# A two-layer encoder trunk with expert retrieval on one core: second-half activations stored in three parts, 20 dense up blocks in place of 26, first splits and gates moved, copies spread

## The chip, the cores and the metric

One core of a Trainium2 chip runs the whole trunk. The metric is the device time of one execution in microseconds; three executions give a median. Its engines work beside each other, each in the order of its own instructions: TensorE (PE in the profile, PEld for its weight loads), VectorE (DVE), ScalarE (ACT), GpSimd (POOL) and SyncE (SP), which here only issues transfers. Sixteen DMA engines carry the transfers.

## The reference, cut to what matters

```python
for i in range(2):                                 # x: 256 tokens x 1024
    m = mla_mixer(x) if i == 0 else dsa_mixer(x)
    x = layernorm(ALPHA * x + m)
    f = peer(x, w_q[i], sub_keys[i], w_down[i], w_up[i])
    x = layernorm(ALPHA * x + f)

def peer(x, w_q, sub_keys, w_down, w_up):          # 16384 experts, 8 heads x 16 picked per token
    s1, s2 = scores of the two halves of x @ w_q against 128 sub-keys each
    expert, gate = top 16 of the 16 x 16 sums of the best 16 of s1 and of s2, softmax
    a = x . w_down[expert]                         # one dot product per token and picked expert
    return sum over picked of gelu(a) * gate * w_up[expert]
```

The 16384 experts are 128 blocks of 128. A token picks at most 128 of 16384.

## The kernel before, in words

**Number format.** Every float32 operand is split in two float16 parts, a high one and the rest (`hi`, `lo` for weights, `xh`, `xl` for activations, made by `Split.high` on ScalarE, L151, and `Split.low` on VectorE, L160). A product is three matmuls, hi·hi, hi·lo and lo·hi. All 128x1024 weight blocks come through one `Stream` in the order of use: `_load` (L199) issues the transfer (a "raw" buffer of a ring of six, on SyncE), then high, then low, some blocks ahead of TensorE.

**Stages of one PEER layer.** The queries (`pq`) and scores (`ps`); the choice of experts on VectorE (`choose`, in pieces between other work); the *down* stage, in which all 128 blocks of `w_down` are multiplied with all 256 tokens (tile `d`, two blocks per step, 24 matmuls of 256 columns each per block) and gelu is put into `A`, a tile [128, 128 blocks, 256 tokens]; and the *up* stage (tile `y`, matmuls of 512 columns).

**Gates.** In the down stage, once the choice is known, `gates` (L1313) turns it, and then 64 groups of four tokens are worked off while the blocks go on: `prepare` (L1380) makes one-hot tiles `hot` on VectorE and `gate` (VectorE or GpSimd and ScalarE), `place` (L1393) multiplies them on TensorE (tile `G`) and multiplies the result into `A` for the four tokens. The same loop counts in `seen` which of the rare blocks are used by which tokens.

**The up stage is not dense.** The first `DENSE` = 26 blocks of `w_up` are multiplied with all tokens. The other 102 (`RARE`) are not: for each of the 128 expert places of a block, the rows of `w_up` that any token of this place uses are listed (`lists`), and 128 rows, one per place, are gathered by an indirect transfer from a DRAM table that holds the row of `w_up` and the 256 activations beside it. 44 such listed items serve both halves of the tokens (12 matmuls of 512 columns each, `JB` + `TB` = 32 + 12), 48 one half (6 matmuls each, `JO` = 24 for each half). `_up_order` sets the order: 20 dense blocks (`HEAD`), then the listed items, with the other 6 dense blocks between them.

**How the table is filled.** The rows of `w_up` are copied from input to table (DRAM to DRAM, 512 KB each, `copies` at L409) behind other loads on SyncE. The activations of the rare blocks are stored by `store` (L1527), four blocks a transfer, in two halves: tokens 0 to 127 from the 32nd group on, tokens 128 to 255 from the 64th group on, which is the end of the down stage. A gather needs the lists, all copies and all stores; its nine buffers also lie on part of `A`, which must have been stored.

**Order.** A scheduler orders the instructions of each engine by its own estimate of times; `tc.issue_after` and the chains of `link` (L455) pin some of it. Transfers issued on SyncE go in order, and each waits until the eighth one before it has landed. `middle_loads` (L1625) fetches the operands of the layer norm (x, gain and bias) half-way through the up items.

Of the kernel before, what the change touches and what calls it, by code (L numbers as in the profile page):

```python
# [16 lines left out]
ALU = mybir.AluOpType  # L17
AX = mybir.AxisListType

P = 128  # L20
T = 256
D = 1024
# [4 lines left out]
NKEYS = 128  # L27
# [38 lines left out]
LEAST, MOST, ROW, SMALL = 64.0, 2.0 ** 40, 4.0, 2.0 ** -24  # L66
BOTH, MOSTLY = 128, 1120
CHECKS = 7 * P
DENSE, HEAD = 26, 20
RARE = P - DENSE  # L70
JB, JO, TB, ROWTAIL = 32, 24, 12, 32
BOTHS = JB + TB
WIDE = D + T
FETCHED, DEEP = 9, 8
LISTED = BOTHS + 2 * JO
END = 6
# [86 lines left out]
class Stream:  # L163
# [35 lines left out]
    def _load(self, upto):  # L199
        while self.n_loaded <= min(upto, len(self.blocks) - 1):  # L200
            src, w, _ = self.blocks[self.n_loaded]
            if self.n_loaded in self.early:
                t = self.early[self.n_loaded]
            elif self.n_loaded in self.rows:
                table, at = self.rows[self.n_loaded]
                t = self.place()
                self.nc.gpsimd.indirect_dma_start(t, None, table, bass.IndirectOffsetOnAxis(ap=at, axis=0))  # L207
# [125 lines left out]
def tile_trunk(ctx: ExitStack, tc: tile.TileContext, ins, out: bass.AP, short, shared):  # L333
    nc = tc.nc
    half = F16 if short else F32R
# [54 lines left out]
    if short:  # L390
        table = [dram.tile([(RARE + 1) * P, WIDE], F32, tag=f"table{i}", name=f"table{i}") for i in range(DEPTH)]
# [17 lines left out]
    def copies(li):  # L409

        down = len(ws.blocks) - NKEYS
        first, few = ((8, 42), (down - 44, 54))[li]
        for n in range(RARE + 1):
            i = first + (down - first) * n // few if n < few else down + 92 * (n - few) // (RARE + 1 - few)
            ws.copied.setdefault(i, []).append((table[li][n * P : (n + 1) * P, :D], ins["up"][li][(DENSE + n) % NKEYS]))

    def add_up(li):
# [91 lines left out]
    def load_x(ar, src):  # L509
        xs = [ar.take(D), ar.take(D)]  # L510
        for t in range(2):
            nc.sync.dma_start(xs[t], src[t])
        return xs

    def rows(o4, lhs, blk, start, stop, tiles=(0, 1)):
# [237 lines left out]

    begun = {}

    def load_affine(ar, li, which):
        g, b = ar.take(D), ar.take(D)
        nc.sync.dma_start(g, ins["ln_gain"][li, which].partition_broadcast(P))
        nc.sync.dma_start(b, ins["ln_bias"][li, which].partition_broadcast(P))
        return g, b  # L760

    def rope(o, p, cos, sin, half, tmp):
# [427 lines left out]
    def peer(li):  # L1190
# [189 lines left out]
        def prepare(g4, engine):  # L1380
            hot = ohp.tile([P, 2, P, 4], F16, tag="V", name="hot")
            gate = ohp.tile([P, 2, 4, P], F16, tag="U", name="gate")
            four = slice(4 * g4, 4 * g4 + 4)
            nc.vector.tensor_tensor(hot, iota4[:, None].to_broadcast([P, 2, P, 4]),  # L1384
                                    place16[:, :, None, four].to_broadcast([P, 2, P, 4]), op=ALU.is_equal)
            engine.tensor_tensor(gate[:, 0], hot[:, 1].rearrange("p c j -> p j c"),  # L1386
                                 gate16[:, four, None].to_broadcast([P, 4, P]), op=ALU.mult)
            for j in range(4):
                t = 4 * g4 + j
                nc.scalar.mul(gate[:, 1, j, :], hot[:, 1, :, j], rest[:, t : t + 1])  # L1390
            onehot[g4] = hot, gate
# [130 lines left out]
                            op0=ALU.mult, op1=ALU.add))  # L1522
            rows_of(up_tail, tail)

        stored = [DENSE, DENSE]

        def store(half, upto):  # L1527

            b0 = stored[half]
            b1 = min(b0 + CHUNKED, NKEYS)  # L1530
            if b0 < b1 <= upto:
                ts = slice(half * P, (half + 1) * P)
                cols = slice(D + half * P, D + (half + 1) * P)
                rows_of = table[li][(b0 - DENSE) * P : (b1 - DENSE) * P, cols].rearrange("(b a) t -> a b t", a=P)
                nc.sync.dma_start(rows_of, A[:, b0:b1, ts])  # L1535
                stored[half] = b1
# [9 lines left out]
        def cut(n):  # L1546
            if n >= len(PAIRED):
                return
            i = PAIRED[n]
            k, slot = ITEMS[i][1], slice(SLOTS[i], SLOTS[i] + 2)  # L1550
            hh, al = xh[:, slot, :], xl[:, slot, :]
            total = split.total("most")
            act(lambda: split.high(hh, A[:, k : k + 2, :], A_UNIT))
            dve(lambda: split.low(al, A[:, k : k + 2, :], A_UNIT, hh, total))
            for j in range(2):
                made[i + j] = hh[:, j, :], al[:, j, :]
# [6 lines left out]
        for b0 in range(0, NKEYS, 2):  # L1563
# [5 lines left out]
                ready = ready or spend(PACE)  # L1569
            if b0 == 0:  # L1570
                chains["pe"] = None
            if short and b0 == NKEYS - 2:
                cut(0)
            t0 = 4 * groups
            if t0 < T:
                nc.scalar.activation(A[:, b0 : b0 + 2, t0:], pv[:, :, t0:], AF.Gelu, scale=1.0 / unit)
# [12 lines left out]
                    prepare(prepared, nc.gpsimd if want == 1 else nc.vector)  # L1589
                    prepared += 1  # L1590
            if short:
                if groups >= 32:
                    store(0, b0)
                    store(0, b0)
                if groups == 64:
                    if listing[0] is None:
                        chains["dve"] = None
                        listing[0] = lists()
                    if b0 < NKEYS - 2:
                        list_on(5)  # L1600
                    for _ in range(3):
                        store(1, b0)
        assert groups == 64, groups
        if not short:
            chains.pop("pe")
# [17 lines left out]
        held = []  # L1623

        def middle_loads():  # L1625
            held.append(load_x(lnar, keep))
            held.append(load_affine(lnar, li, 1))
            if last and short:
                least()
                split.seen = BOTH + split.n["most"]  # L1630
                weigh_up(0, 0, split.seen)

        if short:
            for i, (_, _, tiles) in enumerate(ITEMS):
# [8 lines left out]
                    chains.pop("dve")  # L1643
                    chains.pop("pe")
                if i < HEAD - 8:
                    store(0, NKEYS)
                    store(1, NKEYS)
                    store(1, NKEYS)
                if i == HEAD - 8:
                    assert stored == [NKEYS, NKEYS] and not ws.due, stored  # L1650
                    ws.pieces = 2
                    ws.DMA_AHEAD = DEEP
                if i == len(ITEMS) - 9:
# [176 lines left out]
```

## Time and profile before

| | |
|---|---|
| three runs | 1602.08, 1604.54 (median), 1605.96 us |
| profiled execution | 1601.35 us, of which the program's span is 1599.5 us |
| granted TensorE clock, mean | 0.994 |
| TensorE busy | 1557.4 us (97%) |
| VectorE, ScalarE, GpSimd busy | 1369.6, 1089.2, 379.6 us |
| DMA | 484.28 MB, 303 GB/s on average |
| layer 0: down stage begins, ends | 146 us, 523 us |
| layer 1: down stage ends, last up matmul begins | 1332 us, 1587 us |

Busy time counts a matmul from its start to its modelled end, and neighbours overlap; so the pace of TensorE is read from the number of matmuls in a stretch, and its stalls from stretches in which busy time is short of the stretch.

### The profile page before, as it was taken

To read this page: it belongs to the slowest core of one execution; us is meant where nothing else is said; L and a number is where in the kernel's file an instruction comes from. 1 tells how busy PE (TensorE), PEld (TensorE's weight loads), DVE (VectorE), ACT (ScalarE), POOL (GpSimd) and SP (SyncE) were. 2 spreads that over 40 slices of the span, in tenths; PEclk is the share of its full clock that TensorE was granted. 3 is DMA by queue.
4 is the path that set the end of the run, shared out by engine and by line. 5 is a ranking of instruction groups with operands and counts; after the bars stand their busy time and mean duration, and the time that the engine had idled before them with its cause. 6 is when DMAs were issued, how large, how long until landed. Compare 5 with 4: busy or idle time off the path is not lost.

```text
span 1599.5 us, 33693 instructions
## 1 busy us (share of the span) xinstructions
PE 1557.4 (97%) x12323; PEld 1141.5 (71%) x12323; DVE 1369.6 (86%) x3833; ACT 1089.2 (68%) x1973; POOL 379.6 (24%) x315
## 2 busy tenths in 40 slices
PE   9899999999999999999999999999999999999997
PEld 7669888899999444444578598888999995344443
DVE  7669999999998779878788789989999997698785
ACT  7666666698886457666587667646988873476663
POOL 2001244300000136554032012434000000364440
PEclk9999999999999999999999999999999999999998
DMA  9999889986864999998499998879867659998891
GB/s 378 409 358 361 298 320 331 354 307 209 257 209 155 343 384 374 332 327 326 150 415 408 398 325 291 304 274 323 288 221 229 231 178 277 407 360 311 305 337 51
DMA packets 174447, 484.28 MB, mean 303 GB/s; under 512 B 15040, under 2 KB 68544, under 8 KB 174272
## 3 DMA queue, kind: packets, MB, share of 16 engines
q1 hardware_dynamic: 147488, 360.92, 63.0%
q0 software_dynamic: 26496, 120.60, 20.6%
q8 instruction: 98, 1.61, 0.4%
q14 instruction: 77, 0.63, 0.1%
q10 hardware_dynamic: 288, 0.52, 0.1%
HBM read 450.79 MB, written 139.20 MB: 369 GB/s over the span
## 4 chain that ended last, share of the span: by engine, by line
PE 76%; DVE 11%; DMA 6%; issue 2%; SPq 2%; ACT 2%; DVEq 0%; POOL 0%; POOLq 0%; ACTq 0%
PE d L475 30%; PE y L475 26%; DVE lo L160 6%; PE pq L475 4%; DMA raw<-in_up 4%; PE G L475 4%; PE q L475 3%; PE v L475 2%; PE seen L475 1%; SPq L1535 1%; PE s L475 1%; PE qw L475 1%; ACT hi L151 1%; PE ps L475 1%; DVE arena L1309 1%
## 5 line engine op out<-in xcount | busy, mean ns | idle before, releaser
L475 PE MATMUL d<-xh,lo 128*128 128x256 f16 x2048 | 558.3, 273 | 3.0 <-DVE lo L160 3.0
L475 PE MATMUL d<-xl,hi 128*128 128x256 f16 x2048 | 558.2, 273 | 0.0
L475 PE MATMUL d<-xh,hi 128*128 128x256 f16 x2048 | 558.2, 273 | 0.0
L160 DVE SCALAR_TENSOR_TENSOR lo<-raw,hi 128x1024 f16<-128x1024 f32 (+1 forms) x386 | 473.2, 1235 | 78.9 <-ACT hi L151 73.5
L475 PEld LDWEIGHTS <-hi 128*128 128x128 f16 x5016 | 488.3, 98 | 57.7 <-issue 1.2
L151 ACT ACTIVATE hi<-raw 128x1024 f16<-128x1024 f32 (+1 forms) x366 | 380.7, 1049 | 215.2 <-PE d L475 83.5
L207 POOL DMA_INDIRECT arena<-table,up_at x160 | 179.8, 1124 | 678.7 <-DMA arena<-x 507.4
L475 PEld LDWEIGHTS <-xh 128*128 128x128 f16 x1776 | 172.8, 98 | 211.0 <-issue 8.2
L160 DVE SCALAR_TENSOR_TENSOR lo<-arena,hi 128x512 f16<-128x512 f32 (+1 forms) x366 | 248.4, 716 | 48.2 <-ACT hi L151 47.0
L475 PEld LDWEIGHTS <-lo 128*128 128x128 f16 x2508 | 245.5, 98 | 33.8 <-DVE lo L160 4.9
L475 PE MATMUL y<-hi,xl 128*128 128x512 f16 x816 | 245.5, 380 | 9.2 <-DVE xl L160 9.2
L475 PE MATMUL y<-lo,xh 128*128 128x512 f16 x816 | 246.7, 380 | 2.0 <-DVE lo L160 0.8
L475 PE MATMUL y<-hi,xh 128*128 128x512 f16 x816 | 245.9, 380 | 2.6 <-ACT hi L151 2.6
L151 ACT ACTIVATE hi<-arena 128x1024 f16<-128x1024 f32 x192 | 201.0, 1053 | 39.1 <-issue 21.2
L1390 ACT ACTIVATE gate<-hot,rest 128x128 f16<-128x128 f16 x512 | 167.8, 405 | 13.0 <-DVE hot L1384 10.9
L475 PEld LDWEIGHTS <-xl 128*128 128x128 f16 x888 | 86.2, 98 | 117.8 <-DVE xl L160 14.6
L151 ACT ACTIVATE xh<-arena 128x256 f16<-128x256 f32 (+2 forms) x214 | 87.5, 414 | 86.8 <-PE y L475 61.7
L260 POOL TENSOR_TENSOR lo<-raw,hi 128x1024 f16<-128x1024 f32 x27 | 61.6, 2283 | 192.8 <-ACT hi L258 147.5
L1384 DVE TENSOR_TENSOR hot<-iota,place 128x1024 f16<-128x1024 f16 x128 | 87.6, 689 | 17.1 <-PE G L475 17.0
L160 DVE SCALAR_TENSOR_TENSOR xl<-arena,xh 128x256 f16<-128x256 f32 (+2 forms) x216 | 91.9, 428 | 7.3 <-ACT xh L151 6.9
L475 PE MATMUL G<-gate,hot 128*128 128x128 f16 x1024 | 90.7, 219 | 3.8 <-DVE gate L1386 3.8
L475 PEld LDWEIGHTS <-hot 128*128 128x128 f16 x1536 | 87.8, 113 | 5.0 <-DVE gate L1386 4.3
(261 smaller groups left out, 1811.6 us busy)
## 6 DMA issues: line engine op xcount, KB each, us to landing
raw<-in_down SPq DMA_DIRECT2D x256, 512.0 KB
table<-in_up SPq DMA_DIRECT2D x206, 512.0 KB
raw<-in_up SPq DMA_DIRECT2D x52, 512.0 KB
table<-arena SPq DMA_DIRECT2D x100, 256.0 KB
raw<-in_peer_q SPq DMA_DIRECT2D x24, 512.0 KB
raw<-in_dsa_qk SPq DMA_DIRECT2D x16, 512.0 KB
raw<-in_mla_w_o SPq DMA_DIRECT2D x8, 512.0 KB
arena<-in_peer_q SPq DMA_DIRECT2D x8, 512.0 KB
```

The lines of the kernel that those rows point to most:

```text
L151: return nc.scalar.copy(o, src) if unit == 1.0 else nc.scalar.mul(o, src, unit)
L160: return nc.vector.scalar_tensor_tensor(o, src, unit, hi, op0=ALU.mult, op1=ALU.subtract, accum_out=total)
L207: self.nc.gpsimd.indirect_dma_start(t, None, table, bass.IndirectOffsetOnAxis(ap=at, axis=0))
L260: nc.gpsimd.tensor_tensor(lo, raw, hi if short else hi.bitcast(F32), op=ALU.subtract)
L475: return pe(lambda: nc.tensor.matmul(o, l, r, start=start, stop=stop, skip_group_check=True))
L1309: dve(lambda: nc.vector.tensor_reduce(exp_[t][:, h - 1, :], held, axis=AX.X, op=ALU.add))
L1384: nc.vector.tensor_tensor(hot, iota4[:, None].to_broadcast([P, 2, P, 4]), place16[:, :, None, four].to_broadcast([P, 2, P, 4]), op=ALU.is_ ...
L1390: nc.scalar.mul(gate[:, 1, j, :], hot[:, 1, :, j], rest[:, t : t + 1])
L1535: nc.sync.dma_start(rows_of, A[:, b0:b1, ts])
```

## The change

Seven edits.

1. `DENSE` 26 to 20, `TB` 12 to 16: 20 dense blocks, all ahead of the listed items; 48 items for both halves, 48 for one; 108 rare blocks with a copy and a store each. The up stage has 116 items in place of 118.
2. The activations are stored in four parts (`PARTS`): tokens 0 to 127, 128 to 191, 192 to 223 and 224 to 255, each as soon as its tokens are placed. A stored row is 512, 256, 128 and 128 bytes long.
3. `middle_loads` issues its four transfers on GpSimd's queue, behind the gather that was issued last.
4. The split of the first two dense blocks' activations (`cut(0)`) is issued when the 64th group is placed, and into a spare tile in place of a slot of `xh` and `xl`, which the down stage still reads.
5. The one-hot tiles of groups 1 to 3 wait until the first `gate` has been issued.
6. Copies: fewer ahead of the down stage (24 in place of 42 in layer 0, 46 in place of 54 in layer 1), the others over 108 blocks of the down stage in place of 92.
7. At the end of the down stage three steps of `lists` go with each step in place of five.

```diff
-DENSE, HEAD = 26, 20
+DENSE, HEAD = 20, 20
-JB, JO, TB, ROWTAIL = 32, 24, 12, 32
+JB, JO, TB, ROWTAIL = 32, 24, 16, 32
+PARTS = (0, 128), (128, 192), (192, 224), (224, 256)
...
-        first, few = ((8, 42), (down - 44, 54))[li]
+        first, few = ((12, 24), (down - 44, 46))[li]
...
-            i = first + (down - first) * n // few if n < few else down + 92 * (n - few) // (RARE + 1 - few)
+            i = first + (down - first) * n // few if n < few else down + 108 * (n - few) // (RARE + 1 - few)
...
+            with ExitStack() as order:
+                if short and 0 < g4 < 4:
+                    order.enter_context(tc.issue_after(begun["gate"]))
+                nc.vector.tensor_tensor(hot, iota4[:, None].to_broadcast([P, 2, P, 4]),
+                                        place16[:, :, None, four].to_broadcast([P, 2, P, 4]), op=ALU.is_equal)
...
+            if g4 == 0:
+                begun["gate"] = ins.ins
...
-        def store(half, upto):
+        def store(part, upto):
...
-                ts = slice(half * P, (half + 1) * P)
-                cols = slice(D + half * P, D + (half + 1) * P)
+                ts = slice(*PARTS[part])
+                cols = slice(D + ts.start, D + ts.stop)
...
+            if n == 0:
+                four = spare16.rearrange("p (a b) -> p a b", b=T)
+                hh, al = four[:, 0:2, :], four[:, 2:4, :]
...
-            if short and b0 == NKEYS - 2:
-                cut(0)
...
-                if groups >= 32:
-                    store(0, b0)
-                    store(0, b0)
+                for part, (_, upto) in enumerate(PARTS):
+                    if 4 * groups >= upto:
+                        for _ in range(2 if part == 0 else 3):
+                            store(part, b0)
                 if groups == 64:
                     if listing[0] is None:
                         chains["dve"] = None
+                        cut(0)
                         listing[0] = lists()
                     if b0 < NKEYS - 2:
-                        list_on(5)
-                    for _ in range(3):
-                        store(1, b0)
+                        list_on(3)
...
         def middle_loads():
-            held.append(load_x(lnar, keep))
-            held.append(load_affine(lnar, li, 1))
+            with ExitStack() as order:
+                if short:
+                    order.enter_context(tc.issue_after(ws.fetched))
+                engine = nc.gpsimd if short else nc.sync
+                held.append(load_x(lnar, keep, engine))
+                held.append(load_affine(lnar, li, 1, engine))
```

**The end of layer 0's down stage on SyncE.** In the order before, `128x4x128` is a store of four blocks for 128 tokens. The ten stores in the third row are one of the first half and nine of the second:

```order
L210 DMA raw_7441<-in_up 128x1024
L210 DMA raw_7526<-in_up 128x1024
L1535 DMA table_119<-arena 128x4x128 x10
L210 DMA raw_7556<-in_up 128x1024
L1535 DMA table_119<-arena 128x4x128 x2
L210 DMA raw_7602<-in_up 128x1024
L1535 DMA table_119<-arena 128x4x128 x9
L210 DMA raw_7632<-in_up 128x1024
L1535 DMA table_119<-arena 128x4x128
L210 DMA raw_7676<-in_up 128x1024
L1535 DMA table_119<-arena 128x4x128
L1535 DMA table_119<-arena 128x2x128
```

Now, around the second part, of which the burst begins behind the 48th group (`128x4x64` is a store for 64 tokens):

```order
L1542 DMA table_119<-arena 128x4x128
L1542 DMA table_119<-arena 128x4x64 x9
L212 DMA raw_6875<-in_down 128x1024
L212 DMA raw_6905<-in_down 128x1024
L1542 DMA table_119<-arena 128x4x64 x7
L212 DMA raw_6989<-in_down 128x1024
L1542 DMA table_119<-arena 128x4x64 x3
```

And now behind the 64th group (`128x4x32` is a store for 32 tokens; a like burst of the third part stands between these two pieces, behind the 56th group):

```order
L1542 DMA table_119<-arena 128x4x128
L1542 DMA table_119<-arena 128x4x64
L1542 DMA table_119<-arena 128x4x32 x10
L212 DMA raw_7601<-in_up 128x1024
L1542 DMA table_119<-arena 128x4x32
L212 DMA raw_7648<-in_up 128x1024
L1542 DMA table_119<-arena 128x4x32 x7
L212 DMA raw_7678<-in_up 128x1024
L1542 DMA table_119<-arena 128x4x32
L212 DMA raw_7722<-in_up 128x1024
L1542 DMA table_119<-arena 128x4x32
L1542 DMA table_119<-arena 128x4x128
```

What was one burst of full-width stores behind the 64th group is three bursts, the first two of them among the last loads of the down stage; the last has rows a quarter as long, and x, gain and bias are gone from this queue.

**The first gates on VectorE.** Before, in layer 0:

```order
L1331 TENSOR_TENSOR place_102<-arena 128x256
L1384 TENSOR_TENSOR hot<-iota_106,place_102 128x1024 x4
L1386 TENSOR_TENSOR gate<-hot,gate_103 128x512
L160 SCALAR_TENSOR_TENSOR lo_4048,sums<-raw_3837,hi_4047 128x1024
L1386 TENSOR_TENSOR gate<-hot,gate_103 128x512 x3
```

And now:

```order
L1333 TENSOR_TENSOR place_102<-arena 128x256
L1389 TENSOR_TENSOR hot<-iota_106,place_102 128x1024
L1391 TENSOR_TENSOR gate<-hot,gate_103 128x512
L1389 TENSOR_TENSOR hot<-iota_106,place_102 128x1024 x2
L161 SCALAR_TENSOR_TENSOR lo_4039,sums<-raw_3827,hi_4038 128x1024
```

The first `gate`, which TensorE's first `G` needs, stands behind one `hot` in place of four.

**The first mixer's attention on VectorE.** L812 is the mask and row maximum of the scores `s`; the rows with `lo` split weight blocks (raw_377 and raw_417 those of the values, raw_450 and later ones the mixer's output weights). Before:

```order
L160 SCALAR_TENSOR_TENSOR lo_571,sums<-raw_377,hi_570 128x1024
L781 TENSOR_TENSOR arena<-arena 64x2x256 x2
L160 SCALAR_TENSOR_TENSOR lo_620,sums<-raw_417,hi_619 128x1024
L160 SCALAR_TENSOR_TENSOR lo_656,sums<-raw_450,hi_655 128x1024
L160 SCALAR_TENSOR_TENSOR lo_716,sums<-raw_488,hi_715 128x1024
L160 SCALAR_TENSOR_TENSOR lo_735,sums<-raw_534,hi_734 128x1024
L160 SCALAR_TENSOR_TENSOR lo_955,sums<-raw_574,hi_954 128x1024
L812 ISA arena,m<-s_679,arena 128x128
L812 ISA m 128x1
L812 ISA arena,m<-s_682,arena 128x256
```

And now:

```order
L783 TENSOR_TENSOR arena<-arena 64x2x256 x2
L161 SCALAR_TENSOR_TENSOR lo_725,sums<-raw_526,hi_724 128x1024
L161 SCALAR_TENSOR_TENSOR lo_944,sums<-raw_566,hi_943 128x1024
L814 ISA arena,m<-s_669,arena 128x128
L814 ISA m 128x1
L814 ISA arena,m<-s_672,arena 128x256
L814 ISA m 128x1
L161 SCALAR_TENSOR_TENSOR lo_948,sums<-raw_615,hi_947 128x1024
```

No line of this stage was edited: the scheduler moved the splits, since fewer copies stand ahead of the weights' loads. Before, ScalarE made `hi_734` and `hi_954`, which the last two splits ahead of L812 need, behind its four copies of the values `v`; now the `hi` of every split that stands ahead of the first L812 (L814 in the changed file) comes ahead of these copies.

More of the change, by code (lines that the diff above doesn't have):

```diff
@@ L206, in _load @@
                 t = self.place()
-                self.nc.gpsimd.indirect_dma_start(t, None, table, bass.IndirectOffsetOnAxis(ap=at, axis=0))
+                self.fetched = self.nc.gpsimd.indirect_dma_start(t, None, table,
+                                                                 bass.IndirectOffsetOnAxis(ap=at, axis=0)).ins
             else:
@@ L507, in unscale, with load_x @@
         return nc.scalar.mul(o, p, 1.0 / unit) if short else nc.scalar.copy(o, p)
-    def load_x(ar, src):
+    def load_x(ar, src, engine=nc.sync):
         xs = [ar.take(D), ar.take(D)]
         for t in range(2):
-            nc.sync.dma_start(xs[t], src[t])
+            engine.dma_start(xs[t], src[t])
         return xs
@@ L754, in tile_trunk, with load_affine @@
     begun = {}
-    def load_affine(ar, li, which):
+    def load_affine(ar, li, which, engine=nc.sync):
         g, b = ar.take(D), ar.take(D)
-        nc.sync.dma_start(g, ins["ln_gain"][li, which].partition_broadcast(P))
-        nc.sync.dma_start(b, ins["ln_bias"][li, which].partition_broadcast(P))
+        engine.dma_start(g, ins["ln_gain"][li, which].partition_broadcast(P))
+        engine.dma_start(b, ins["ln_bias"][li, which].partition_broadcast(P))
         return g, b
@@ L1383, in prepare @@
             four = slice(4 * g4, 4 * g4 + 4)
[L1384 to L1387, printed above, removed]
+            with ExitStack() as order:
[3 more added lines that the diff above has]
+                                        place16[:, :, None, four].to_broadcast([P, 2, P, 4]), op=ALU.is_equal)
+            ins = engine.tensor_tensor(gate[:, 0], hot[:, 1].rearrange("p c j -> p j c"),
+                                       gate16[:, four, None].to_broadcast([P, 4, P]), op=ALU.mult)
+            if g4 == 0:
+                begun["gate"] = ins.ins
             for j in range(4):
@@ L1523, in lists @@
             rows_of(up_tail, tail)
-        stored = [DENSE, DENSE]
-        def store(half, upto):
-            b0 = stored[half]
+        stored = [DENSE] * len(PARTS)
+        def store(part, upto):
+            b0 = stored[part]
             b1 = min(b0 + CHUNKED, NKEYS)
             if b0 < b1 <= upto:
-                ts = slice(half * P, (half + 1) * P)
-                cols = slice(D + half * P, D + (half + 1) * P)
+                ts = slice(*PARTS[part])
+                cols = slice(D + ts.start, D + ts.stop)
                 rows_of = table[li][(b0 - DENSE) * P : (b1 - DENSE) * P, cols].rearrange("(b a) t -> a b t", a=P)
                 nc.sync.dma_start(rows_of, A[:, b0:b1, ts])
-                stored[half] = b1
+                stored[part] = b1
         listing = [None]
@@ L1645, in peer @@
                 if i < HEAD - 8:
-                    store(0, NKEYS)
-                    store(1, NKEYS)
-                    store(1, NKEYS)
+                    for part in range(len(PARTS)):
+                        store(part, NKEYS)
+                    store(part, NKEYS)
                 if i == HEAD - 8:
-                    assert stored == [NKEYS, NKEYS] and not ws.due, stored
+                    assert stored == [NKEYS] * len(PARTS) and not ws.due, stored
                     ws.pieces = 2
```

## The prediction

> **What bounds the kernel.** I read the page's busy shares and slices first, then a table of stretches, then who waits for whom where TensorE is short.
>
> ```profile
> PE 1557.4 (97%) x12323; PEld 1141.5 (71%) x12323; DVE 1369.6 (86%) x3833; ACT 1089.2 (68%) x1973; POOL 379.6 (24%) x315
> PE   9899999999999999999999999999999999999997
> DMA  9999889986864999998499998879867659998891
> PE 76%; DVE 11%; DMA 6%; issue 2%; SPq 2%; ACT 2%; DVEq 0%; POOL 0%; POOLq 0%; ACTq 0%
> ```
>
> TensorE is busy nearly everywhere and carries 76% of the chain that ended last. So a matmul less is time less, wherever TensorE does not wait. The table of stretches says where it waits (us of the stretch, then busy us of PE, PEld, DVE, ACT, POOL, then clock, DMA share, GB/s):
>
> ```profile
> 36.00:62.00 26.00, 20.37 (x118) 15.40 (x118) 19.90 (x57) 20.07 (x40) 3.32 (x3) 0.87 1.03 411
> 140.00:300.00 160.00, 159.55 (x1460) 142.75 (x1459) 155.06 (x465) 102.61 (x127) 61.48 (x39) 1.00 0.90 316
> 300.00:320.00 20.00, 18.34 (x187) 16.44 (x186) 19.27 (x40) 14.67 (x32) 0.00 (x0) 1.00 1.00 392
> 412.00:517.00 105.00, 105.00 (x1165) 96.37 (x1163) 96.07 (x171) 83.17 (x217) 0.00 (x0) 1.00 0.67 215
> 517.00:582.00 65.00, 57.63 (x303) 28.96 (x301) 43.96 (x137) 26.80 (x36) 11.71 (x9) 1.00 1.01 358
> 600.00:760.00 160.00, 160.00 (x748) 72.57 (x746) 134.92 (x508) 111.19 (x162) 83.65 (x76) 1.00 0.92 339
> 1040.00:1100.00 60.00, 57.41 (x521) 50.30 (x519) 54.97 (x136) 33.40 (x42) 27.13 (x19) 1.00 0.82 283
> 1100.00:1120.00 20.00, 17.88 (x170) 15.84 (x169) 19.90 (x38) 10.69 (x21) 3.67 (x2) 1.00 0.98 349
> 1320.00:1400.00 80.00, 73.57 (x411) 37.86 (x408) 56.59 (x176) 35.19 (x51) 14.86 (x13) 0.98 0.97 343
> ```
>
> TensorE is short by 5.6 us in the first mixer's attention (36 to 62), 1.7 and 2.1 us where the gates begin (300 to 320, 1100 to 1120), 2.6 us in layer 1's down stage, and 7.4 and 6.4 us where the down stage gives way to the up stage (517 to 582, 1320 to 1400). In the listed part of the up stage (600 to 760) it never waits, with the DMA engines at 0.92. The releasers, from the waits of 240 to 320, 36 to 62, 515 to 600 and 1318 to 1400 in this order (engine and line, what it waited for: us, times, longest):
>
> ```profile
> PE G L475 <- DVE gate L1386: 1.7, 1, 1.7
> ...
> PE s L475 <- DVE m L812: 4.5, 1, 4.5
> ...
> ACT hi L151 <- DMA raw<-in_up: 31.2, 12, 7.5
> PE y L475 <- DVE xl L160: 4.7, 4, 2.5
> ...
> ACT hi L151 <- DMA raw<-in_up: 31.7, 12, 7.3
> PE y L475 <- DVE xl L160: 4.5, 3, 2.5
> ```
>
> **Fewer dense blocks.** Per layer 6 dense items of 12 matmuls go and 4 listed items of 12 come: 24 matmuls of 512 columns less, 48 in both layers. Their pace is in the stretch of tile y alone, and the two rows behind it price 6 more columns of `seen`:
>
> ```profile
> 600.00:760.00 160.00, 159.96 (x742) 0.00 (x0) 1.00 0.92 339
> ...
> L475 PE MATMUL G<-gate,hot x1024: 219/219/247, 312.5 to 1321.5; 128*128 128x128 f16 x171
> ...
> L475 PE MATMUL seen<-gate,hot x512: 208/208/208, 312.6 to 1321.4; 128*128 128x102 f16 x171
> ```
>
> 159.96 / 742 = 0.2156 us each: -10.35 us. 26 columns are 11 ns, 6 are 2.5 ns, times 512: +1.3 us. That holds if gathers keep up. Before, 184 gathers and 12 interleaved dense loads feed the listed parts; now 192 gathers of 640 KB in a stretch that is 3% shorter, so some 345 GB/s for 339, where 411 GB/s stands in the first row of the table. I cost it at nothing. Splits are cover here too: VectorE has 134.92 of 160 us, and per item nothing changes.
>
> **First gates.** VectorE's timeline at 309 us:
>
> ```profile
> 309.38 2.50 DVE L1384 TENSOR_TENSOR hot<-iota,place 128x1024 f16<-128x1024 f16 x4
> 311.79 0.68 DVE L1386 TENSOR_TENSOR gate<-hot,gate 128x512 f16<-128x512 f16 x1
> ```
>
> Three of four `hot` move behind the gate: 3 x 0.6 = 1.8 us, against idles of 1.7 and 2.1 us. Taken: -1.7 and -1.8, -3.5 us.
>
> **Early first split.** The longest wait of `y` for `xl` is 2.5 us in each layer: the first `xh` can be written only when the last `d` has read its slot. With the spare tile it is made some blocks sooner: -5.0 us, hidden in VectorE's time before the stage's end (96.07 of 105 us). The fewer list steps there make room.
>
> **Stores in parts.** Behind the wait for `xl`, the rest of the shortfall, 4.9 + 3.9 = 8.8 us, is loads of dense up blocks that come late (31 us of ScalarE's waits in each layer). Their cause is the burst of stores:
>
> ```profile
> DMA packets 13733, 8.67 MB, mean 299 GB/s; under 512 B 463, under 2 KB 13216, under 8 KB 13731
> ...
> table<-arena SPq DMA_DIRECT2D x26, 256.0 KB
> raw<-in_up SPq DMA_DIRECT2D x5, 512.0 KB
> ```
>
> This is 517 to 546 us: 29 x 16 = 464 engine-us. 515 packets of 4 KB at 411 GB/s over 16 engines are 159 ns each, 82 us; the rest, over 13216 rows of 512 bytes, is 28.5 ns a row: 0.91 us per store, 23.7 us for 26. 512 bytes at that rate are 20 ns, so a straight line says 8.6 ns plus bytes: 18.6 ns for 256, 13.6 ns for 128 bytes, 0.60 and 0.44 us per store. No row shows a short row written to DRAM; the ends are by bytes alone (10 and 5 ns) and as dear as 512 bytes (28.5). I take the line, as two sizes lie on it. Then 412 to 517 us, with 0.33 x 105 = 35 us of free engines, takes the second part (27 x 0.60 = 16.1), the third (11.7), one more first store and three late copies (0.9 + 3 x 1.28): 32.5 us. It just fits, with up to six raw buffers filled ahead. Behind the last group 11.7 us of stores stand in place of 23.7, and the four operand loads (4 x 1.28 = 5.1) are gone: 17 us less of 65, against 7.4 us of idle. The lists come later (13 steps, 3 at a time and then 1) and gathers wait for them; but the first gather was issued here,
>
> ```profile
> 551.15 1.27 POOL L207 DMA_INDIRECT arena<-table,up_at  x1 [253.46 <-DMA arena<-x]
> ```
>
> held by the stores, and it is needed behind 20 dense items, 20 x 12 x 0.2156 = 52 us after the 523 us at which the down stage ends. A delay of the lists by some 6 us costs nothing. I take -7.5 of the 8.8; ends -8.8 and +8 (first rival).
>
> [...]
>
> **First mixer.** VectorE waits 4.5 us for ScalarE's `hi` ahead of L812, and TensorE behind L812 for 4.5 us; both engines' orders no longer put these `hi` behind the copies of `v`, and 18 fewer copies lie ahead of the weights. What is late next is the softmax itself. Ends 0 and -5.6; nearest is the row of 4.5, less what other steps take back: -3.
>
> **Copies.** Layer 0's down stage before the gates gets 0.79 copies a block for 0.67:
>
> ```profile
> raw<-in_down SPq DMA_DIRECT2D x58, 512.0 KB
> table<-in_up SPq DMA_DIRECT2D x39, 512.0 KB
> ```
>
> That is 7 more in 140 to 300 us, 9 us of DMA, share 0.90 to 0.95, with VectorE at 155.06 of 160 us, so that a late block is not caught up. Ends 0 and +6 (the 5% of 160 us less the spare); +2 with layer 1.
>
> **Operand loads on GpSimd.** Four issues stand between gathers, priced by the nearest row:
>
> ```profile
> L207 POOL DMA_INDIRECT arena<-table,up_at x160: 935/1023/1988, 551.1 to 1557.1; - x160
> ```
>
> Some 1 us of GpSimd and 1.28 us of DMA each, 5 us once per layer, ahead of 14 and more gathers; nine buffers of about 1.95 us per item (7.76 us per four) cover it partly. GpSimd has 83.65 of 160 us. Ends 0 and +4: +1 us.
>
> **Sum.** -10.35 + 1.3 - 3.5 - 5.0 - 7.5 - 3 + 2 + 1 = -25 us. The profiled execution took 1601.35 us (span 1599.5 and 1.85 around it); its successor is 1576.3. The profiled execution lies 3.2 us under the median of the three, 1604.54, and 0.7 under the fastest; I add 1.7 and give 1578 as the median to come.
>
> **Rivals.** First: short rows cost as much as 512-byte rows. Then 412 to 517 us gets 27 x 2 x 0.91 + 4.7 = 54 us for 35 free, 19 us are carried past 517, the last burst stays 24.6 us; less 5.1 for the operands and 6.4 for five loads not needed there: +8 us a layer, in place of the gains of stores and early split. Sum: -10.35 + 1.3 - 3.5 - 3 + 3 + 16 = +3.5, so 1604.8, as a median 1606. For it: the rows' cost is partly fixed. Against: two sizes on one line.
>
> [...]
>
> Third: the price is right but the DMA engines, at 0.95 before the gates and full to 32.5 of 35 us behind them, run late, or GpSimd's issues delay gathers. Then copies +6, stores -2 in place of -7.5, loads +4: 1601.35 - 25 + 4 + 5.5 + 3 = 1588.9, as a median 1590.5. For it: 0.82 to 0.90 already has ScalarE waiting for `in_down`. Against: 411 GB/s is sustained elsewhere.
>
> **Chances.** Forecast 0.62 (1578), third 0.18 (1590.5), first 0.12 (1606), second 0.08 (1645). The forecast and the third are faster; of the first I count 0.04 faster, 0.06 within 0.2%, 0.02 slower. 0.2%, some 3.2 us, is about what a measurement of this kernel tells from no change. Faster 0.84, within 0.06, slower 0.10. The range: below, all shortfall of these places gone, 1601.35 - 10.35 + 1.3 - 3.5 - 13.8 - 5.6 = 1569; above, 1600, between the third and the first. The likeliest case's own range is 1569 to 1586.
>
> **What would show it.** Right: 24 fewer `y` matmuls a layer; no idle of `G` above 0.5 us; no wait of the first `y` for its activations; DMA share between the 32nd group and the end of the down stage near 1 with TensorE still full; short-row stores at 0.4 to 0.6 us in a burst; `s` no longer held 4.5 us by L812. Wrong: TensorE idle inside the gate phase (rows too dear), stretches of the down stage ahead of the gates short of TensorE (copies), or `xh` waiting long for gathers half-way through the up stage (operand loads).

## The result, and the profile after

The changed kernel takes 1576.9 us (median; 1574.99 to 1579.19), the kernel before 1603.8 (1602.08 to 1605.96) on the same chip: a ratio of 0.9832, 95% interval 0.9814 to 0.9851. The forecast was 1578. The profiled execution took 1576.3 us (span 1574.4), 25.05 us under the one of before; the sum had said 25. The sum is right, but not all of its parts, as the rest shows.

From the page after, the busy times, the slices of PE and DMA, and the chain's shares by engine:

```profile
span 1574.4 us, 33700 instructions
...
PE 1544.1 (98%) x12275; PEld 1136.9 (72%) x12275; DVE 1362.9 (87%) x3823; ACT 1081.9 (69%) x1968; POOL 386.0 (25%) x330
...
PE   9999999999999999999999999999999999999996
...
DMA  9898899998989999998499978889878899899992
...
PE 82%; DVE 9%; DMA 3%; issue 2%; ACT 2%; SPq 1%; POOL 0%; DVEq 0%; POOLq 0%; ACTq 0%
```

48 matmuls fewer are there. DMA and VectorE have lost share on the chain to TensorE. The stretches (us of the stretch; busy us of PE, PEld, DVE, ACT, POOL; granted clock; DMA share; GB/s):

```profile
36.00:62.00 26.00, 25.82 (x173) 21.15 (x172) 23.46 (x86) 25.30 (x65) 3.56 (x4) 1.00 1.03 416
140.00:300.00 160.00, 158.15 (x1442) 140.48 (x1441) 150.26 (x447) 94.76 (x120) 60.20 (x38) 1.00 0.93 333
300.00:320.00 20.00, 19.22 (x203) 17.22 (x200) 19.24 (x39) 16.85 (x41) 0.00 (x0) 1.00 1.03 418
412.00:517.00 105.00, 105.00 (x1153) 96.28 (x1151) 95.58 (x173) 81.96 (x211) 0.00 (x0) 1.00 0.91 265
517.00:582.00 65.00, 61.30 (x294) 28.84 (x292) 48.91 (x159) 30.54 (x41) 15.86 (x13) 0.97 1.00 324
600.00:760.00 160.00, 160.00 (x743) 72.50 (x741) 133.08 (x494) 111.19 (x161) 80.99 (x80) 1.00 0.88 330
1100.00:1120.00 20.00, 19.50 (x215) 17.57 (x214) 18.86 (x35) 17.09 (x43) 0.00 (x0) 1.00 1.00 386
1320.00:1400.00 80.00, 77.14 (x415) 36.12 (x413) 63.18 (x212) 42.62 (x59) 26.26 (x23) 1.00 0.91 292
```

TensorE's shortfall went from 5.6 to 0.2 us in the first mixer, from 1.7 and 2.1 to 0.8 and 0.5 us at the first gates, from 7.4 and 6.4 to 3.7 and 2.9 us where the down stage ends; it rose from 0.45 to 1.85 us ahead of the gates. Between 412 and 517 us the DMA share went from 0.67 to 0.91 and TensorE waits for nothing.

What is left at the end of the down stage is one wait per layer. The waits of 515 to 600 us (what waited, for what: us, times, longest), then VectorE's, ScalarE's and SyncE's timelines there:

```profile
ACT hi L152 <- DMA raw<-in_up: 21.2, 10, 6.5
...
DVE arena L1587 <- ACT d L1586: 6.5, 1, 6.5
...
PE y L477 <- DVE xl L161: 3.7, 1, 3.7
```

```profile
528.92 0.69 DVE L1587 TENSOR_TENSOR arena<-arena,d 128x512 f32<-128x512 f32 x1 [6.50 <-ACT d L1586]
529.53 0.68 DVE L161 SCALAR_TENSOR_TENSOR xl<-arena,xh 128x512 f16<-128x512 f32 x1
```

```profile
527.35 1.06 ACT L152 ACTIVATE hi<-raw 128x1024 f16<-128x1024 f32 x1 [6.49 <-DMA raw<-in_up]
528.31 0.58 ACT L1586 ACTIVATE d<-d 128x512 f32<-128x512 f32 x1
```

```profile
507.63 0.45 SPq L212 DMA_DIRECT2D raw<-in_up  x1
508.13 5.74 SPq L1542 DMA_DIRECT2D table<-arena  x9
513.97 0.45 SPq L212 DMA_DIRECT2D raw<-in_up  x1
514.52 8.69 SPq L1542 DMA_DIRECT2D table<-arena  x12
523.32 0.45 SPq L212 DMA_DIRECT2D raw<-in_up  x1
```

Read from the bottom: an up block is loaded at 523.32, behind nine and twelve stores; its `hi` on ScalarE waits 6.49 us for it; the last block's gelu (L1586) is queued behind this `hi`, VectorE's multiplication (L1587) behind the gelu, and the second pair's `xl` behind that. TensorE waits 3.7 us. The first pair has its operands (`spare`), but the wait it was rid of has moved one pair on.

### The profile page after: what moved, and what is told of

Its sections match the earlier page's. It is cut to its first block, busy times and chain, and to the rows that moved or that the text cites. A ratio compares the mean times of both kernels' runs of the same rounds, so it can differ in the third digit from the quotient of the medians.

```text
span 1574.4 us, 33700 instructions
## 1 busy us (share of the span) xinstructions
PE 1544.1 (98%) x12275; PEld 1136.9 (72%) x12275; DVE 1362.9 (87%) x3823; ACT 1081.9 (69%) x1968; POOL 386.0 (25%) x330
## 4 chain that ended last, share of the span: by engine, by line
PE 82%; DVE 9%; DMA 3%; issue 2%; ACT 2%; SPq 1%; POOL 0%; DVEq 0%; POOLq 0%; ACTq 0%
PE y L477 32%; PE d L477 30%; PE pq L477 4%; DVE lo L161 4%; PE G L477 4%; PE q L477 3%; DMA raw<-in_down 2%; PE v L477 2%; PE seen L477 2%; ACT hi L152 1%; SPq L1542 1%; PE qw L477 1%; PE ps L477 1%; PE h L477 1%; DVE arena L1311 1%
## 5 line engine op out<-in xcount | busy, mean ns | idle before, releaser
L161 DVE SCALAR_TENSOR_TENSOR lo<-raw,hi 128x1024 f16<-128x1024 f32 (+1 forms) x363 | 455.0, 1261 | 52.4 <-ACT hi L152 49.7
L152 ACT ACTIVATE hi<-raw 128x1024 f16<-128x1024 f32 (+1 forms) x355 | 368.1, 1048 | 171.5 <-PE d L477 63.5
L477 PEld LDWEIGHTS <-xh 128*128 128x128 f16 x1712 | 166.6, 98 | 199.0 <-ACT xh L152 3.0
L161 DVE SCALAR_TENSOR_TENSOR lo<-arena,hi 128x512 f16<-128x512 f32 (+1 forms) x382 | 259.2, 715 | 45.2 <-ACT hi L152 44.5
L477 PE MATMUL y<-hi,xl 128*128 128x512 f16 x784 | 236.5, 380 | 6.6 <-DVE xl L161 6.6
L477 PE MATMUL y<-lo,xh 128*128 128x512 f16 x784 | 236.5, 380 | 0.0
L477 PE MATMUL y<-hi,xh 128*128 128x512 f16 x784 | 236.1, 380 | 0.0
L152 ACT ACTIVATE hi<-arena 128x1024 f16<-128x1024 f32 x200 | 209.1, 1052 | 14.3 <-PE y L477 3.9
L152 ACT ACTIVATE xh<-arena 128x256 f16<-128x256 f32 (+1 forms) x214 | 86.7, 407 | 116.8 <-PE y L477 74.9
L1307 POOL TENSOR_TENSOR arena<-arena 128x800 f32<-128x800 f16 x32 | 73.3, 2290 | 73.1 <-DVE arena L1304 62.6
```

The lines of the kernel that those rows point to most:

```text
L152: return nc.scalar.copy(o, src) if unit == 1.0 else nc.scalar.mul(o, src, unit)
L161: return nc.vector.scalar_tensor_tensor(o, src, unit, hi, op0=ALU.mult, op1=ALU.subtract, accum_out=total)
L477: return pe(lambda: nc.tensor.matmul(o, l, r, start=start, stop=stop, skip_group_check=True))
L1307: nc.gpsimd.tensor_tensor(o.rearrange("p k c -> p c k"), same, cell[t][:, h, :, None].to_broadcast([P, CELLS, TOPK]), op=ALU.mult)
```

## The experiments

Every kernel starts from the changed one. Times are medians, ratios are to the kernel before on the same chip. "Slower" and "faster" are against the 1576.9 us of the changed kernel, which was measured in another series; how far two series lie apart is seen below (**One store of the last part per step**): some 2 us by the medians, 4 us by the ratios.

**Stores in two parts.**

```diff
-PARTS = (0, 128), (128, 192), (192, 224), (224, 256)
+PARTS = (0, 128), (128, 256)
```

> The changed kernel with the second half stored in one part again (512-byte rows, only when every gate is placed); all else as changed. If stores in three parts bring what the prediction took for them (7.5 us in both layers), the time is 1577 + 7.5 = 1584.5 us, and up to 1587 if the wait of the second pair for `xl`, which stands behind a late load of an up block, grows with the longer burst; the DMA share in the stage that ends the down stage is then low ahead of the end and the burst behind it some 24 us long. Rival: the gain at the change of stages is that of the operand loads and the early split, and the stores only fill free DMA time: within 1 us of 1577. Rival of costs: if short rows were dearer than the line, undoing them would make the kernel faster, under 1576.

1584.9 us, ratio 0.9872 (0.9852 to 0.9891): 8.0 us slower. The stretch of 412 to 517 us falls back to a DMA share of 0.71 (the eighth column):

```profile
412.00:517.00 105.00, 105.00 (x1161) 96.33 (x1160) 95.18 (x168) 82.73 (x214) 0.00 (x0) 1.00 0.71 235
```

That is near the term for the stores (7.5), but its interval almost touches the changed kernel's (0.9814 to 0.9851). The trace has the loss in the right place: where the down stage ends TensorE is idle for 3.4 us more (60.18 of 65 us between 517 and 582, for 61.30; 74.88 of 80 between 1320 and 1400, for 77.14), and the clock of the latter stretch is 0.96 for 1.00, some 3 us more. It also loses 2.0 us between 140 and 300 us, where no store of this part stands.

**26 dense blocks.**

```diff
-DENSE, HEAD = 20, 20
+DENSE, HEAD = 26, 20
-JB, JO, TB, ROWTAIL = 32, 24, 16, 32
+JB, JO, TB, ROWTAIL = 32, 24, 12, 32
```

> The changed kernel with 26 dense blocks and 12 tail items again; all else as changed. By count, 48 y matmuls of 0.2156 us come back and 6 columns of `seen` go: +10.35 - 1.3 = +9.05, 1586 us. Rival: the gathers of 192 items had been late or near it, so that part of the count was paid back somewhere: then undoing gives clearly less, under 1583. Rival: fewer list steps and one store group less also shorten the change of stages: 1584 with shorter waits for `xl`.

1585.2 us, 0.9879 (0.9861 to 0.9896): 8.3 slower for 9.05 by count. The time can't tell this from the last rival (1584 with shorter waits), and the trace has some of it: between 1320 and 1400 us TensorE has all 80 us, where the changed kernel waits 2.9 us for `xl`; layer 0 waits 3.7 us as there.

**Copies where they were.**

```diff
-        first, few = ((12, 24), (down - 44, 46))[li]
+        first, few = ((8, 42), (down - 44, 54))[li]
-  ... down + 108 * (n - few) // (RARE + 1 - few)
+  ... down + 92 * (n - few) // (RARE + 1 - few)
```

> The changed kernel with the copies placed as before (first 8, few 42 and 54, 92); all else as changed. By the trace of the changed kernel the first mixer gained some 7 us and the down stages lost 3 against the prediction's 3 and 2. If both come from the place of the copies: +7 - 3 = +4, 1581 us, with TensorE short by 5 to 6 us again in the attention between 36 and 62 us. By the prediction's sizes: +3 - 2 = +1, 1578. Rival: the first mixer's gain is not the copies' (the order of the engines moved for another reason): 1574, 3 us faster.

1580.6 us, 0.9856 (0.9839 to 0.9873): 3.7 slower, which the intervals do not tell from nothing. In the trace the stretch of 36 to 62 us and its longest wait of TensorE come back to the digit:

```profile
36.00:62.00 26.00, 20.37 (x127) 15.49 (x125) 20.00 (x57) 19.99 (x40) 3.31 (x3) 0.93 1.03 411
```

```profile
PE s L477 <- DVE m L814: 4.5, 1, 4.5
```

So it is the copies alone that held the first mixer's attention. They are worth 5.4 us of idle there, and more: the clock is not full behind the wait (0.93). In return the changed kernel's down stages are short by more: TensorE has 158.15 us between 140 and 300 us and 96.45 between 1000 and 1100, here 160.00 and 99.48. These two stretches vary by themselves, though: a second trace of the same order of instructions (**One store of the last part per step**) has 159.00 and 98.63.

**Late first split.**

```diff
-            if n == 0:
-                four = spare16.rearrange("p (a b) -> p a b", b=T)
-                hh, al = four[:, 0:2, :], four[:, 2:4, :]
...
+            if short and b0 == NKEYS - 2:
+                cut(0)
...
-                        cut(0)
                         listing[0] = lists()
```

> The changed kernel with the first split made where it was before (in the slot that the last d block reads), all else as changed. By the prediction's term the first pair waits 2.5 us again in each layer: +5.0, 1582 us. Rival, by the trace of the changed kernel: TensorE now waits 3.9 and 3.0 us in front of the second pair, for an `xl` queued behind the last block's gelu, which is queued behind a `hi` whose load is late; a wait in front of the first pair then only comes ahead of the same late work, and the time is 1577, within 1 us. The sum of idle ahead of the first and second pair tells them apart: 3 to 4 us by the rival, 5.5 to 6.5 by the prediction, per layer.

1572.2 us, 0.9798 (0.9782 to 0.9814): 4.7 us *faster* than the changed kernel. Neither theory had that. The scheduler had answered the edit on another queue:

```profile
510.44 0.45 SPq L212 DMA_DIRECT2D raw<-in_up  x1
510.93 5.84 SPq L1542 DMA_DIRECT2D table<-arena  x9
516.88 0.45 SPq L212 DMA_DIRECT2D raw<-in_up  x1
517.43 6.43 SPq L1542 DMA_DIRECT2D table<-arena  x8
523.96 0.45 SPq L212 DMA_DIRECT2D raw<-in_up  x1
```

Eight stores for twelve stand ahead of the late load. Against the first `y` (522.98 us here, 520.38 there) the load is issued 1.0 us later, where it was 2.9, and TensorE waits twice for 0.9 us. It has 63.34 of 65 us between 517 and 582 (for 61.30) and 79.26 of 80 between 1320 and 1400 (for 77.14), so the gain lies where the stages change. That makes a new theory: what counts is how many stores stand ahead of that load.

**First gates as before, and operand loads on SyncE,** each by itself, in one series with two others.

```diff
-                if short and 0 < g4 < 4:
+                if False:
```

> The changed kernel with the four first `hot` in front of the first `gate` again; all else as changed. By the prediction +3.5 us, 1580.5; by the idles in the two traces (before 1.7 and 2.1 us ahead of the first `G`, after 0.45 and 0.1 with 0.7 at the second) +2.2 to 2.5 us, 1579.3. Rival: the idle is made up by whatever TensorE would have waited for next: within 1 us of 1577. What stands in the trace decides between the first two: the longest wait of `G` for `gate` in each layer, 1.7 to 2.1 us or more.

```diff
-                    order.enter_context(tc.issue_after(ws.fetched))
-                engine = nc.gpsimd if short else nc.sync
+                engine = nc.sync
```

> The changed kernel with the four operand loads of the norm issued by SyncE half-way through the up stage, as before; all else as changed. By the prediction GpSimd's issues cost 1 us: 1576, no difference that can be measured. By the trace of the changed kernel they cost nothing (TensorE never waits in the listed part): 1577. Rival: on SyncE the loads are issued far ahead, in the burst of stores (the queue is then free of other work), and take 5.1 us of a full DMA at the change of stages in each layer: 1580 to 1584, with longer waits of `hi` for `in_up` and a later first gather.

1580.6 us (0.9864, 0.9844 to 0.9884) and 1582.5 us (0.9862, 0.9841 to 0.9882). In the same series the changed kernel's own order of instructions ran again (next but one): 1579.1. Against that it is 1.5 and 3.4 us, and by the ratios less than 1: times do not tell either from nothing. For the gates the trace does; the longest waits of `G` in the two layers are back, 1.6 and 1.7 us. For the operand loads it does not: SyncE issues them from 550 us on, 20 us behind the load at 530.25 us that all wait for, so that the longer wait for `xl` (5.0 us in layer 0, for 3.7) is not theirs, and the largest loss of that execution, 5.95 of 160 us between 140 and 300 us, lies far ahead of them. The waits of `G`:

```profile
PE G L477 <- DVE gate L1391: 1.6, 1, 1.6
...
PE G L477 <- DVE gate L1391: 1.7, 1, 1.7
```

**Parts of 32 tokens.**

```diff
-PARTS = (0, 128), (128, 192), (192, 224), (224, 256)
+PARTS = (0, 128), (128, 160), (160, 192), (192, 224), (224, 256)
```

> The changed kernel with the second half stored in four parts of 32 tokens (128-byte rows) in place of 64, 32 and 32. By the straight line a store of 64 tokens of 0.60 us becomes two of 0.44: +0.28 x 27 = 7.6 us of DMA per layer ahead of the end of the down stage, where the shares of the changed kernel leave about 9 us free, and 27 more issues on SP: 1577 to 1581. If a short row cost as much as a 512-byte row, two stores would take 1.82 us where 0.91 stood, +24 us a layer, carried into the up stage: 1600 or more. If the cost were by bytes, 1577 and a DMA share no higher than before. Mean time of a packet and the share of the stretch from 412 to 520 us tell it.

1597.05 us, 0.996 (0.995 to 0.997): 20 us slower (18 against the changed order in the same series), far over the 4 I allowed by the line, and less than half of what the 512-byte price makes (2 x 24). That price is out by the packets too: between 514 and 523 us of this trace 5239 packets under 512 bytes, 512 of 512 bytes and 243 larger ones kept the 16 DMA engines busy for 129 us (0.895 of 9 us), which at the changed kernel's 27 and 159 ns for the other two leaves an estimate of 14.6 ns for a short one; the 128-byte packets of the changed kernel took 13 ns. The late load on SyncE's timeline, VectorE's row behind it, and TensorE's wait:

```profile
515.31 7.88 SPq L1542 DMA_DIRECT2D table<-arena  x9
523.28 0.45 SPq L212 DMA_DIRECT2D raw<-in_up  x1
523.78 8.75 SPq L1542 DMA_DIRECT2D table<-arena  x14
532.64 0.44 SPq L212 DMA_DIRECT2D raw<-in_up  x1
```

```profile
538.38 0.69 DVE L1587 TENSOR_TENSOR arena<-arena,d 128x512 f32<-128x512 f32 x1 [11.94 <-ACT d L1586]
```

```profile
PE y L477 <- DVE xl L161: 8.5, 1, 8.5
```

The load goes out at 532.64 for 523.32, 9.3 us later, and the kernel is 9 to 10 us slower per layer. Part of that is the slower clock behind the longer waits: its mean is 0.89 between 517 and 582 us and 0.94 between 1320 and 1400, for 0.97 and 1.00. My expectation had taken the 9 us of free DMA time ahead of the end for usable. The share of 412 to 517 us rose only from 0.91 to 0.94, 3 of the 7.6 us; so the rest seems to land in the burst, in front of the one load that all wait for.

**One store of the last part per step.**

```diff
-                        for _ in range(2 if part == 0 else 3):
+                        for _ in range((2, 3, 3, 1)[part]):
```

> The changed kernel with the last part stored once per block pair of the down stage in place of three times (the rest follows two per dense item, as now). Theory: TensorE's waits of 3.9 and 3.0 us in front of the second pair come from loads of up blocks that stand on SyncE behind some twenty short stores, which hold `hi`, behind it the last block's gelu on ScalarE and the cuts on VectorE. Then eight stores fewer stand ahead of that load, 8 x 0.56 = 4.5 us, the wait goes or shrinks below 1 us, and the time is 1577 - 6 = 1571 (the waits with what is lost behind them are 5.5 and 3.0 us). Rival: the load is late because the raw buffers come free late (DMA_AHEAD, AHEAD), not for the stores: 1577, with the same wait. Rival: the stores left for the dense items hold the gathers: TensorE waits half-way through the up stage, 1580.

1579.1 us, 0.9858 (0.9836 to 0.9879), the same wait. But the edit did nothing: the scheduler filled SP's queue as before, and on every engine the instructions stand in the same order as in the changed kernel. So this run says nothing on the theory; it is a second measurement of the changed kernel, and shows how far two series lie apart (0.9832 and 0.9858, 0.0026 or some 4 us). Against this one, by the ratios, the stores in two parts cost 2 us, the 26 blocks 3, the copies nothing, and the late split gains 10. So a difference of 4 us or less between series is settled by the traces or not at all.

**Stores held behind loads.** This edit does move them:

```diff
-                nc.sync.dma_start(rows_of, A[:, b0:b1, ts])
+                with ExitStack() as order:
+                    if part > 1:
+                        order.enter_context(tc.issue_after(ws.last))
+                    nc.sync.dma_start(rows_of, A[:, b0:b1, ts])
```

> The changed kernel with each store of the third and fourth part held behind the last load of a weight block that the program had issued before it (the scheduler had moved these stores ahead of loads; the order of SP now shows 3, 0, 3, 3 and 6 short rows' stores behind the first up loads, where 6, 3, 7, 10 and 1 stood). Theory: the wait for the second pair's `xl` at the change of stages is that of a load behind stores on SyncE. Then the load that is issued at 523.3 us comes some 11 stores x 0.55 = 6 us sooner, the waits of 3.9 and 3.0 us (5.5 and 3.0 with what is lost behind them) go or fall under 1 us, and the time is 1577 - 6 = 1571 us, or 1570. Rival: the raw buffers free late and the load can't be issued earlier; SyncE then only idles and the stores end later: 1577 to 1580 with the same wait. Rival: the stores, later in sum, hold the gathers: TensorE waits half-way through the up stage (after 570 us).

1570.5 us (1569.99 to 1570.96), 0.98 (0.9787 to 0.9814): as the theory said. SyncE's timeline (from the load before the late one) and the waits of `y` from 515 to 600 us:

```profile
508.17 0.45 SPq L212 DMA_DIRECT2D raw<-in_up  x1
512.18 2.68 SPq L1545 DMA_DIRECT2D table<-arena  x5
517.47 0.35 SPq L212 DMA_DIRECT2D raw<-in_up  x1
```

```profile
PE y L477 <- ACT hi L152: 1.0, 1, 1.0
...
PE y L477 <- DVE lo L161: 0.5, 2, 0.2
```

The late load goes out at 517.47, 5.9 us sooner, and the wait for `xl` is gone. The two stretches in which the down stages end:

```profile
517.00:582.00 65.00, 64.86 (x321) 31.14 (x320) 50.23 (x159) 29.57 (x38) 13.48 (x13) 1.00 0.99 298
...
1320.00:1400.00 80.00, 80.00 (x429) 37.61 (x428) 66.33 (x227) 44.17 (x62) 28.47 (x27) 1.00 0.98 306
```

That is 3.6 and 2.9 us more of TensorE than in the changed kernel, 6.4 together, and the median is 6.4 us lower. No gather holds TensorE (160.00 of 160 us between 600 and 760).

**The late split on top of it.** The edits of the two runs together.

> As the run with the stores held behind loads, and the first split made as late as before. If the late split's gain of 4.7 us came only from four stores that the scheduler no longer put ahead of the same load (6 for 10 in SP's order), that gain is gone here: the first pair waits for `xl` again, up to 2.5 us in each layer, and the time is equal to the other run's or up to 5 us above it (1571 to 1576). If the late split gains by itself (by the order of ScalarE and VectorE), it is 4 to 5 us below the other run: 1567.

1571.15 us, 0.9807 (0.9793 to 0.982): 0.7 above the run before. With the stores out of the way the place of the first split is worth nothing that can be measured, one way or the other; TensorE waits 0.9 us for the first pair's `xl` in each layer again. So the 4.7 us go with the four stores.

**Copies in the pause.** On top of that:

```diff
-        first, few = ((12, 24), (down - 44, 46))[li]
+        first, few = ((12, 31), (down - 44, 54))[li]
+            if li == 0 and n < few:
+                i = 12 + n if n < 14 else 26 if n < 22 else 27 + n - 22
...
-                for o, i in self.due[:2]:
+                for o, i in self.due[: 10 if self.n_loaded == 26 else 2]:
```

> As the run before (stores behind loads, late split), with copies moved: in layer 0, 31 in place of 24 ahead of the down stage, eight of them issued together at 57 us, ahead of the stretch from 62 to 78 us in which SyncE issues no load and the DMA engines stand free; 78 for 85 behind; in layer 1, 54 and 55 for 46 and 63. If the down stages' losses (2.0 us in layer 0 and 4.4 in layer 1's 1000 to 1100 us) come from copies on a full DMA, some 3 to 4 us go: 3.5 us below the run before. If the first mixer pays them back (its attention waits for `hi` again), no difference, or up to 5 us slower, with TensorE short between 36 and 90 us.

1568.3 us, 0.9784 (0.9771 to 0.9797), 2.8 under the run before and the best here; 8.6 under the changed kernel. The first mixer keeps its gain, and 1000 to 1100 us has 99.68 us of TensorE, where the run before has 98.19 with a clock of 0.98 (some 2 us more). Between 140 and 300 us nothing is gained: 157.61 us for 157.94. So the gain fits layer 1's part of the expectation, and not layer 0's. Its rows:

```profile
36.00:62.00 26.00, 25.82 (x176) 21.11 (x174) 23.28 (x83) 25.08 (x63) 3.55 (x4) 1.00 1.02 407
...
1000.00:1100.00 100.00, 99.68 (x918) 89.01 (x917) 94.92 (x213) 57.17 (x75) 43.67 (x25) 1.00 0.87 307
```

**Operand loads again, where nothing else waits.** The stores held behind loads, with the loads on SyncE (both edits above).

> The run with the stores held behind loads (1570.5 us, its five times within 1 us), with the four operand loads of the norm issued by SyncE again. There the change of stages holds no other wait, so that the loads' own price shows. If putting them on GpSimd is worth what the looser comparison seemed to say (some 3 to 5 us), 1574 to 1575, with TensorE waiting for dense up blocks between 550 and 600 us. If it is worth nothing either way: 1570.5 within 1 us. By the prediction, that GpSimd's issues cost 1 us: 1569.5.

1574.3 us (1571.32 to 1577.95), 0.9817 (0.9797 to 0.9837): 3.8 above its base, but the intervals overlap. In the profiled execution layer 0 has no idle between 517 and 582 us, and layer 1 waits for a `hi` (3.0 us) behind a late `in_up`. That the move to GpSimd costs 1 us is not borne out; that it gains some 3 is likely and not settled.

## Why the prediction was right, point by point

- **Fewer dense blocks** (-9.05): right by the count of the page (48 matmuls fewer). 8.3 came back with the 26, within the spread of the series; `seen` has 128x108 columns, and the listed part still holds TensorE at 160.00 of 160 us. That gathers cost nothing holds, with 330 GB/s.
- **Stores in parts** (-7.5): right in its price, and near in size as far as the series tell (8.0 by undoing it). The single packets in the trace of the changed kernel took 13 ns (128 bytes), 18 (256), 27 (512) and 159 (4 KB) in the median; the line had said 13.6, 18.6 and 28.5. The first rival (a short row as dear as 512 bytes) falls with that. No run shows the price behind the second rival's 1645 us, a short row dearer than one of 512 bytes: 18 and 13 ns stand beside 27. The four times lie near one straight line (8.3 ns plus 1 ns for every 27 bytes), and a packet of 256 or 128 bytes took 0.67 or 0.48 of the time of one of 512. A slip in the working changes nothing: 382 us over 13216 rows are 28.9 ns, not 28.5.
- **Early first split** (-5.0): this step failed. I took the longest wait of `y` for `xl` and removed it, and did not ask what is late next: the second pair's `xl`, behind the last gelu, behind a `hi`, behind a load, behind stores. Nor did I look at what the scheduler makes of SP's queue once the split is emitted elsewhere: four more stores ahead of that load. In the changed kernel the step costs 4.7 us by the medians, and without those stores nothing.
- **First mixer** (-3): the mechanism right, the size off. It gave 5.4 us of idle, nearly my outer end of 5.6, and the clock between 20 and 60 us rose from 0.92 to 1.00, up to 40 x 0.08 = 3 us more. I had taken the middle, and had priced a stall at its idle without the slow matmuls behind it.
- **Copies** (+2): right in the trace of the changed kernel (1.4 us of idle more than before between 140 and 300 us, 1.0 more between 1000 and 1100), but not shown: the second trace of the same order has 0.55 more and 1.2 less. Mixer and copies undone together cost 3.7, where the forecast had 1.
- **First gates** (-3.5): right in kind, and smaller. The idle of the two stretches fell from 3.8 to 1.3 us, -2.5; a wait of 0.5 us for the second group (L1418) remains.
- **Operand loads** (+1): no cost. TensorE waits nowhere half-way through the up stage (160.00 of 160 us between 600 and 760), and the third rival's GpSimd is refuted there. A gain is not shown either.

Within the two traces, the count (-9.05) and the idles (-7.2 where the down stage ends, for -12.5 in the sum; -5.4, -2.5 and +2.4) make -21.8 of the 25.05 us; what is left, 3.3 us, is about the slow clock's share: by its means in these stretches an estimate of 40 x 0.08 + 80 x 0.02 - 65 x 0.03 = 2.9 us. By undoing, the six add up to 8.0 + 8.3 + 3.7 - 4.7 + 3.7 + 5.6 = 24.6 of 26.9 us, each with the spread of the series. So that the sum came out to the microsecond is luck in part: the end of the down stage gave 5.3 us less than was forecast there, and the first mixer, with its clock, about that much more. The third rival had its place right (the end of the down stage, loads that come late), though not its size: the DMA engines were busy 0.91 of 105 us ahead of the end, and what came late was one load per layer, behind a burst of stores.

## What to carry to other kernels

A long wait that is removed is worth only the distance to the next late thing on the same chain; follow that chain through every queue (here PE, VectorE, ScalarE, SyncE) before taking the whole wait. In a queue that is served in order, ask of each bulk transfer which urgent load stands behind it: changing only the order, with not a byte less to move, gave 6.4 us here. And where a scheduler places instructions, read its order after each edit, since an edit on two engines moved stores on a third, and another moved nothing at all.

## What was not expected of the hardware

An idle of TensorE cost more than itself here. TensorE's timeline of the changed kernel, with one wait of 3.70 us, and the clock in the stretch behind it:

```profile
525.99 0.59 PE L477 MATMUL y<-lo,xh 128*128 128x512 f16 x2
530.28 1.03 PE L477 MATMUL y<-hi,xl 128*128 128x512 f16 x2 [3.70 <-DVE xl L161]
531.11 1.06 PE L477 MATMUL y<-hi,xh 128*128 128x512 f16 x2
...
533.67 0.62 PE L477 MATMUL y<-hi,xh 128*128 128x512 f16 x2
```

```profile
530.20:534.00 3.80, 3.72 (x10) 1.41 (x11) 3.73 (x13) 0.18 (x1) 0.00 (x0) 0.55 0.98 214
```

Two matmuls take 1.03 to 1.06 us for 0.59 until 533.67, 3.4 us: eight at 0.43 in place of 0.2156, 1.7 us lost beyond the 3.7. The granted clock has a mean of 0.55 between 530.2 and 534 us, and of 1.00 in the 4 us behind. The length of one wait does not tell by itself where this happens: in layer 1 of the same execution the clock stays full behind a wait of 2.9 us (1.00 between 1320 and 1400 us), while in the kernel before it is halved for 3.4 us from 1364 us on (0.61 on the mean between 1364 and 1368.4 us), behind three waits of 0.28, 0.68 and 0.92 us that follow each other within 3.1 us. So a slow stretch of 3.4 us stood behind one long wait in the one kernel, and behind three short ones in the other; what sets it off is not shown.
